# Source order for VectorE and ScalarE in the gated-input stage of a hybrid conformer layer, a softmax in two steps, and key and bias loads two heads ahead

## The chip, the cores and the metric

The kernel runs on one core of one Trainium2 chip. The time is device microseconds of one execution; the median of three runs of the kernel before is 1996.45 us (1996.19 to 1996.85). The engines are called as the profile calls them: PE (TensorE, matrix products), PEld (its weight loads), DVE (VectorE), ACT (ScalarE), POOL (GpSimd) and SP (SyncE, which here only issues DMAs).

## The reference

One layer of a streaming encoder, for a prompt of 256 frames and for 8 running streams of 16 new frames with 128 past frames each. Both share the weights.

```python
def hybrid_layer(x, conv_buf, ffn_buf, attn_fn, ...):
    h = rmsnorm(x, norm_mix_g)
    proj = h @ w_in            # [GLU in | q | k | v | forget logits | gate A | gate B]
    ...
    u = glu_in[..., :D_CONV] * jax.nn.sigmoid(glu_in[..., D_CONV:])
    ext = jnp.concatenate([conv_buf.astype(u.dtype), u], axis=1)
    z = layernorm(causal_dwconv(ext, conv_dw_w, conv_dw_b), conv_ln_g, conv_ln_b)   # 31 taps
    a_out = (z * jax.nn.sigmoid(z)) @ conv_pw_out
    q = rmsnorm(q, q_norm_g)
    k = rmsnorm(k, k_norm_g)
    logf = jax.nn.log_sigmoid(f_logit + b_forget)
    b_out = attn_fn(q, k, v, logf) @ w_att_out
    x = x + (gate_a * a_out + gate_b * b_out) @ w_out
    h2 = rmsnorm(x, norm_ffn_g)
    up = h2 @ w_up
    ...
    x = x + (jax.nn.silu(gc) * u_half) @ w_down
```

`attn_fn` is causal attention over 8 heads of 128 features. To each score a bias of summed log forget gates is added, and the softmax runs over the keys. The prompt is swept in two blocks of 128 queries; the 128 sample rows see their past keys (`cache_k`) and their own.

## The kernel before, in words

**Tokens and products.** The 256 + 128 = 384 tokens are three tiles of 128 rows. Every fp32 operand of a product is split into hi + lo, and each product is three matmuls (L245 to L247 with the weights stationary). Weights stream in as tiles `raw` of two 128-row blocks x 512 columns: SP issues the DMA (L139), ACT casts the high part `hi` (L148), and DVE forms the low part `lo` = raw - hi (L149). Of `raw`, `hi` and `lo` there are three buffers each.

**The gated-input stage.** `gemm` computes the GLU columns in four panels of 16 k-steps: 64 steps, 0 to 63. One weight tile serves two steps. At the first step of a tile, `ahead(3)` emits the fetch and split of the tile that is used two tiles later, so the split emitted at step 14 is used at steps 18 and 19. A panel ends at steps 15, 31, 47 and 63; its four PSUM results are evacuated by `glu_evac`: two by a DVE multiplication into `sgb` (L706) and a sigmoid on ACT (L707), which needs an ACT table load, two by a DVE multiplication into `ut` (L710), which POOL multiplies by `sgb` (L711).

**Beside it.** After each step, `tick` advances two generators.
- `attention()`: head h issues `head_operands` at step 6h + 6 (kTs, a DVE transposition of its past keys, L611, and qz, a DVE copy of its sample queries, L617), `head_scores` at 6h + 9, `head_probs` at 6h + 14, `head_out` at 6h + 17 and `head_last` at 6h + 19. `head_scores` fills three PSUM buffers s0 (L622), s1 (L624) and s2 (L626, and L630 against the past keys), adds the bias on DVE with the row's maximum (L636), negates (L638), and exponentiates on ACT (L639); before the change it also takes the reciprocal of the sum (L640, DVE) and scales (L641, ACT). `head_probs` transposes the probabilities on PE and copies them out of PSUM: pT on ACT (L650), pz on DVE (L653). `head_out` makes the outputs `on` (L665) and `attT` (L670), `head_last` the second `attT` (L676).
- `conv()`: the depthwise convolution, a chunk of 128 channels at a time, one DVE instruction for each of the 31 taps (L752, L754). Chunks overlap, so that in some steps two taps fall; `fill` (L731 to L737) builds a chunk's input, `load_state` fetches it.

**PSUM.** Products accumulate in five `acc` buffers; everything else rotates through three `misc` buffers. The scores of head h + 1 come one step behind `head_probs` of head h (steps 14 and 15, 20 and 21, 26 and 27, and so on to 50 and 51), and they take the buffers that `head_probs` leaves: s1 (L624) needs the one that pT (L650) reads, s2 (L626) the one that pz (L653) reads.

**What sets the order.** PE's order is written by hand: the order of the source. On the other engines a scheduler places instructions by priority, which is the source position less an offset: 150 for fetches and splits (SPLIT_AHEAD), 250 for the attention's steps (ATT_AHEAD), 400 for evacuations (EVAC_AHEAD). `queued(d)` ties an instruction behind the last queued one of its engine, without a wait. Key loads (`load_k`, four DMAs of a quarter each, two buffers) run one head ahead, bias loads (`load_b`, four DMAs) two. All loads, fetches among them, share SP's one queue, and each DMA waits there until its buffer is free.

Of the kernel before, what the change touches and what calls it, by code (L numbers as in the profile page):

```python
# [33 lines left out]
SPLIT_AHEAD, ATT_AHEAD, EVAC_AHEAD = 150, 250, 400  # L34
# [6 lines left out]
def hybrid_step(  # L41
# [70 lines left out]
    def newton_rsqrt(r, s, m):  # L112
        queued(nc.scalar.activation(s, m, AF.Sqrt), in_first())
        nc.vector.reciprocal(r, s)
# [31 lines left out]
    def split_rows(hi, lo, raw, o, k):  # L146
        first = in_first()
        queued(nc.scalar.copy(hi[:, k, :o], raw[:, k, :o]), first)  # L148
        queued(tt(lo[:, k, :o], raw[:, k, :o], f(hi[:, k, :o]), op=ALU.subtract), first)  # L149
# [77 lines left out]
    def gemm(jobs, sides=(), wide=False):  # L227
        for js in jobs:
# [4 lines left out]
            for j, k in [(j, k + i) for k in range(0, js[0]["nk"], 2) for j in js for i in range(2)]:  # L233
# [29 lines left out]
    def blocks(rows, put):  # L263
        src = rows.rearrange("p t (m b j) -> p b m t j", m=4, b=4)
        for b in range(4):
            for a in range(4):
                nc.vector.transpose(put(a, slice(32 * b, 32 * b + 32)), src[32 * a:32 * a + 32, b])  # L267
# [22 lines left out]
    def x_chunk(c):  # L290
# [5 lines left out]
        with tc.high_priority(offset=EVAC_AHEAD):  # L296
            queued(nc.scalar.activation(hi, ps[:, :NT], AF.Identity, scale=g))  # L297
# [4 lines left out]
    with tc.manual_schedule(engines={ENG.SP, ENG.Activation, ENG.DVE}):  # L302
        nc.vector.memset(junk[:, 0:1], 0.0)
        nc.scalar.dma_start(gm_row[:], norm_mix_g[0].rearrange("(c p) -> c p", p=P))
        nc.scalar.activation(junk[:, 1:2], junk[:, 0:1], AF.Identity)
# [16 lines left out]
        nc.vector.tensor_copy(gm[:], pv[:, :16])  # L322
# [17 lines left out]
    def over_partitions(dg, dst):  # L340
# [3 lines left out]
        nc.scalar.copy(dst, ps[:, :NT])  # L344
# [46 lines left out]
    def small_columns():  # L391
        ps = misc_tile()
        tr(ps[:, :R_N], vrow[:R_N, :], ident[:R_N, :R_N])
        nc.vector.tensor_copy(col[:], ps[:, :R_N])
        ts(qgs[:], col[:, R_QG:R_QG + 1], float(P) ** -0.5, None, op0=ALU.mult)

    def first_norm():
        for c in range(2, 16, 2):
# [6 lines left out]
            if c % 4 == 2:  # L405
                for t in range(NTT):
                    n = c // 4
                    sq = nc.scalar.activation(junk[:], xs[n][:, t, :], AF.Square, accum_out=ssx[:, t, n:n + 1])
# [9 lines left out]
        with tc.high_priority(offset=EVAC_AHEAD):  # L418
            nc.vector.tensor_reduce(mt[:], ssx[:], axis=mybir.AxisListType.X, op=ALU.add)
            ts(mt[:], mt[:], 1.0 / DM, EPS, op0=ALU.mult, op1=ALU.add)  # L420
            r = rsqrt(mt[:], [P, NTT], p_x0, "r1")
            nc.vector.tensor_copy(rs1[:], r[:])
# [14 lines left out]
    def tok_job(dst, c0, n, sq):  # L437
        d = job("B", 16, ha, tok_evac(dst, c0, n))

        def post():  # L440
            for t in range(NTT):
                for h in range(c0 // P, (c0 + n) // P):
                    jk = p_qkv.tile([P, P], F32, tag="jk", bufs=2, name="jk")
                    nc.scalar.activation(jk[:], dst[:, t, h * P:(h + 1) * P], AF.Square,
# [4 lines left out]
    def tok_evac(dst, c0, n, shared=True):  # L449
        def ev(t, ps):  # L450
            if shared and t % 2:
                ts(dst[:, t, c0:c0 + n], ps[:, :n], rs1[:, t:t + 1], None, op0=ALU.mult)
            else:
                queued(nc.scalar.activation(dst[:, t, c0:c0 + n], ps[:, :n], AF.Identity, scale=rs1[:, t:t + 1]),
# [16 lines left out]
    nc.scalar.activation(e[:], e[:], AF.Exp, scale=-1.0)  # L471
    ts(r[:], e[:], 2.0, None, op0=ALU.add)
    nc.vector.reciprocal(r[:], r[:])
# [27 lines left out]
    def bias_rows():  # L501
        for _ in range(6):
            yield
        for i in range(2):
# [3 lines left out]
            nc.vector.tensor_copy(cw[:, i * 124:(i + 1) * 124], ps[:, :124])  # L508
            nc.vector.tensor_copy(fw[:, i * 66:(i + 1) * 66], ps[:, 128:128 + 66])
# [5 lines left out]
        nc.scalar.activation(crow[:, :2 * P], ps[:H, :2 * P], AF.Copy, scale=-1.0)  # L515
        ps = misc_tile()
        mm(ps[:H, :P], lg[:, 2, :], bm[:], start=True, stop=True)
        nc.scalar.activation(crow[:, 2 * P:], ps[:H, :P], AF.Copy, scale=-1.0)
# [3 lines left out]
        nc.scalar.copy(drow[:], ps[:64, :P])  # L522
# [18 lines left out]
    def q_panel(n):  # L541
        blocks(qt[:, :, 512 * n:512 * (n + 1)], by_feature(attT[:, 4 * n:4 * n + 4]))
        for h in range(4 * n, 4 * n + 4):
            nc.scalar.activation(attT[:, h], attT[:, h], AF.Identity, scale=qgs[:])
# [64 lines left out]
    def head_past_keys(d):  # L609
        kTs = p_att.tile([P, 8, P], F32, tag="kTs", bufs=1, name="kTs")  # L610
        nc.vector.transpose(kTs[:].rearrange("p b k -> p (b k)"), kcs[d["h"]][:])  # L611
        d["kTs"] = kTs

    def head_operands(d):
        head_past_keys(d)
        d["bs"] = bss[d["h"]]
        nc.vector.tensor_copy(qz[d["h"] % 2][:, :, :, 0:16], by_stream(attT[:, d["h"], 2 * P:]))  # L617

    def head_scores(d):
# [14 lines left out]
        for i, (sp_, o, n) in enumerate(segs):  # L634
            v = pr[:, o * P:(o + n) * P]
            nc.vector.tensor_tensor_reduce(out=v, in0=sp_[:, :n * P], in1=bs[:, o * P:(o + n) * P], scale=1.0,  # L636
                                           scalar=-3.0e38, op0=ALU.add, op1=ALU.max, accum_out=mx[:, i:i + 1])
            ts(mx[:, 3 + i:4 + i], mx[:, i:i + 1], -1.0, None, op0=ALU.mult)  # L638
            nc.scalar.activation(v, v, AF.Exp, bias=mx[:, 3 + i:4 + i], accum_out=mx[:, 6 + i:7 + i])  # L639
            nc.vector.reciprocal(mx[:, i:i + 1], mx[:, 6 + i:7 + i])  # L640
# [466 lines left out]
```

## Time and profile before

| | us |
|---|---|
| median of 3 runs | 1996.45 |
| the profiled execution | 1998.56 |
| its span | 1996.7 |
| mean granted clock of PE | 0.999 |
| DVE, all additions of the split, L149 (x481) | 580.5 |
| ACT, all casts of the split, L148 (x481) | 496.3 |
| DVE, taps, L754 (x240) | 151.9 |

The profile is of one execution, so its times are set against 1998.56 and not against the median. A row of the timeline gives the start in us from the span's start, the length, the engine, the line, the operation, the output and inputs, and in brackets how long the engine had been idle and what released it. A window's row gives the busy time and instruction count of PE, PEld, DVE, ACT and POOL, then PE's granted clock (1.00 is full speed), the busy share of the 16 DMA engines (which can pass 1 where packets are counted together at an edge) and GB/s.

### The profile page before, as it was taken

To read this page: it belongs to the slowest core of one execution; us is meant where nothing else is said; L and a number is where in the kernel's file an instruction comes from. 1 tells how busy PE (TensorE), PEld (TensorE's weight loads), DVE (VectorE), ACT (ScalarE), POOL (GpSimd) and SP (SyncE) were. 2 spreads that over 40 slices of the span, in tenths; PEclk is the share of its full clock that TensorE was granted. 3 is DMA by queue.
4 is the path that set the end of the run, shared out by engine and by line. 5 is a ranking of instruction groups with operands and counts; after the bars stand their busy time and mean duration, and the time that the engine had idled before them with its cause. 6 is when DMAs were issued, how large, how long until landed. Compare 5 with 4: busy or idle time off the path is not lost.

```text
span 1996.7 us, 24449 instructions
## 1 busy us (share of the span) xinstructions
PE 1986.5 (99%) x9383; PEld 1676.0 (84%) x9383; DVE 1305.3 (65%) x1908; ACT 743.2 (37%) x1077; POOL 89.5 (4%) x216
## 2 busy tenths in 40 slices
PE   9999999999999999999999999999999999999999
PEld 9888999888888888888888888888888888888887
DVE  4455889788755487676867683377673376638663
ACT  5535354433334433344333432233332233323321
POOL 1000011100000000000000000010000000000000
PEclk9999999999999999999999999999999999999999
DMA  6564767444443334534344443444433444343443
GB/s 184 149 188 117 216 154 161 141 140 131 130 129 124 128 125 163 165 122 137 119 137 126 129 134 129 129 126 127 136 129 132 132 118 137 128 133 120 138 158 106
DMA packets 209254, 275.98 MB, mean 138 GB/s; under 512 B 55878, under 2 KB 96729, under 8 KB 209129
## 3 DMA queue, kind: packets, MB, share of 16 engines
q1 hardware_dynamic: 208817, 273.85, 46.0%
q8 instruction: 73, 1.20, 0.3%
q0 software_dynamic: 288, 0.57, 0.1%
q14 instruction: 44, 0.36, 0.1%
q10 hardware_dynamic: 32, 0.01, 0.0%
HBM read 266.98 MB, written 7.86 MB: 138 GB/s over the span
## 4 chain that ended last, share of the span: by engine, by line
PE 96%; DVE 2%; DMA 1%; issue 0%; SPq 0%; ACT 0%; DVEq 0%; ACTq 0%
PE acc L252 20%; PE acc L250 20%; PE acc L251 20%; PE misc L252 10%; PE misc L251 10%; PE misc L250 10%; PE acc L245 2%; PE acc L247 2%; PE acc L246 2%; DVE lo L149 1%; DMA raw<-in_w_in_dram 0%; DVE mixT L267 0%; DVE ut L754 0%; DMA vc<-in_cache_v_dram 0%; DMA bs<-c_dr 0%
## 5 line engine op out<-in xcount | busy, mean ns | idle before, releaser
L149 DVE TENSOR_TENSOR lo<-raw,hi 128x1024 fp32r<-128x1024 f32 (+2 forms) x481 | 580.5, 1207 | 530.7 <-ACT hi L148 526.8
L148 ACT CAST hi<-raw 128x1024 fp32r<-128x1024 f32 (+2 forms) x481 | 496.3, 1032 | 970.1 <-PE misc L252 841.1
L250 PE MATMUL acc<-hi,xg 128*128 128x512 f32 x704 | 274.9, 390 | 0.0
L252 PE MATMUL acc<-hi,xg 128*128 128x512 f32 x704 | 273.9, 389 | 0.0
L251 PE MATMUL acc<-lo,xg 128*128 128x512 f32 x704 | 273.9, 389 | 0.0
L250 PE MATMUL acc<-hi,hT 128*128 128x512 f32 (+1 forms) x512 | 193.0, 377 | 0.5 <-ACT hT L297 0.5
L252 PE MATMUL acc<-hi,hT 128*128 128x512 f32 (+1 forms) x512 | 190.4, 372 | 0.2
L251 PE MATMUL acc<-lo,hT 128*128 128x512 f32 (+1 forms) x512 | 190.3, 372 | 0.0
L250 PEld LDWEIGHTS acc<-hi,xg 128*128 128x128 f32 x704 | 132.1, 188 | 28.4
L754 DVE SCALAR_TENSOR_TENSOR ut<-ext,cw,ut 128x384 f32<-128x384 f32 x240 | 151.9, 633 | 6.0
L252 PEld LDWEIGHTS acc<-hi,xg 128*128 128x128 f32 x704 | 132.1, 188 | 27.5
L251 PEld LDWEIGHTS acc<-lo,xg 128*128 128x128 f32 x704 | 132.2, 188 | 27.1
L252 PE MATMUL misc<-hi,xg 128*128 128x512 f32 x352 | 137.0, 389 | 0.0
L250 PE MATMUL misc<-hi,xg 128*128 128x512 f32 x352 | 137.0, 389 | 0.0
L251 PE MATMUL misc<-lo,xg 128*128 128x512 f32 x352 | 136.9, 389 | 0.0
L250 PE MATMUL acc<-hi,act 128*128 128x512 f32 x352 | 136.9, 389 | 0.0
L251 PE MATMUL acc<-lo,act 128*128 128x512 f32 x352 | 136.9, 389 | 0.0
L252 PE MATMUL acc<-hi,act 128*128 128x512 f32 x352 | 136.9, 389 | 0.0
L267 DVE STREAM_TRANSPOSE extf<-tok 32x384 f32<-32x384 f32 x176 | 100.3, 570 | 30.9 <-ACT tok L988 28.2
L267 DVE STREAM_TRANSPOSE uT<-tok 32x384 f32<-32x384 f32 x176 | 100.3, 570 | 29.7 <-ACT tok L988 26.9
L250 PEld LDWEIGHTS acc<-hi,hT 128*128 128x128 f32 x512 | 96.2, 188 | 16.1 <-ACT hT L297 1.0
L252 PEld LDWEIGHTS acc<-hi,hT 128*128 128x128 f32 x512 | 96.1, 188 | 15.7 <-DVE hT L298 0.7
(325 smaller groups left out, 3133.8 us busy)
## 6 DMA issues: line engine op xcount, KB each, us to landing
raw<-in_w_up_dram SPq DMA_DIRECT2D x176, 512.0 KB
raw<-in_w_in_dram SPq DMA_DIRECT2D x96, 512.0 KB
raw<-in_w_down_dram SPq DMA_DIRECT2D x88, 512.0 KB
raw<-in_w_in_dram SPq DMA_DIRECT2D x64, 256.0 KB
raw<-in_w_out_dram SPq DMA_DIRECT2D x32, 512.0 KB
raw<-in_w_att_out_dram SPq DMA_DIRECT2D x16, 512.0 KB
raw<-in_conv_pw_out_dram SPq DMA_DIRECT2D x16, 512.0 KB
raw<-in_w_in_dram SPq DMA_DIRECT2D x23, 344.0 KB
```

What stands on the lines that cost most here:

```text
L148: queued(nc.scalar.copy(hi[:, k, :o], raw[:, k, :o]), first)
L149: queued(tt(lo[:, k, :o], raw[:, k, :o], f(hi[:, k, :o]), op=ALU.subtract), first)
L245: mm(o, hi[:, kk, s], ah, start=st, stop=False)
L246: mm(o, hi[:, kk, s], al, start=False, stop=False)
L247: mm(o, lo[:, kk, s], ah, start=False, stop=sp)
L250: mm(o, ah[:, s], hi[:, kk, :n], start=st, stop=False)
L251: mm(o, ah[:, s], lo[:, kk, :n], start=False, stop=False)
L252: mm(o, al[:, s], hi[:, kk, :n], start=False, stop=sp)
L267: nc.vector.transpose(put(a, slice(32 * b, 32 * b + 32)), src[32 * a:32 * a + 32, b])
L754: stt(o, v, wc, o, op0=ALU.mult, op1=ALU.add)
```

## The change

Four things change, and PE's order not at all.
- `dve` and `act` wrap VectorE and ScalarE. While the list `chained` isn't empty, each of their instructions is `queued`, that is, keeps its place in the source. The list is filled before the gated-input stage and emptied behind `drain(att_steps)`; evacuations in `gemm` are exempt. In the profile of the changed kernel all these instructions bear the line of the wrapper, L89.
- The softmax goes in two steps: `head_scores` ends with the exponentials, and a new `head_scale` at step 6h + 10 takes one reciprocal of three columns in place of three of one, and scales three times.
- The attention's steps lose their priority offset (ATT_AHEAD).
- Keys are loaded two heads ahead instead of one, bias loads move from `head_probs` to `head_scale`; these, the value loads and the convolution's state get the offset of the splits.

```diff
-SPLIT_AHEAD, ATT_AHEAD, EVAC_AHEAD = 150, 250, 400
+SPLIT_AHEAD, EVAC_AHEAD = 150, 400
...
+    chained = []
+
+    class InOrder:
+        def __init__(self, eng):
+            self.eng = eng
+
+        def __getattr__(self, name):
+            op = getattr(self.eng, name)
+
+            def call(*a, **kw):
+                d = op(*a, **kw)
+                if chained:
+                    queued(d)
+                return d
+            return call
+
+    dve, act = InOrder(nc.vector), InOrder(nc.scalar)
...
-    tt = nc.vector.tensor_tensor
-    stt = nc.vector.scalar_tensor_tensor
-    ts = nc.vector.tensor_scalar
+    tt = dve.tensor_tensor
+    stt = dve.scalar_tensor_tensor
+    ts = dve.tensor_scalar
...
                 if sp:
+                    held, chained[:] = chained[:], []
                     with tc.high_priority(offset=EVAC_AHEAD):
-                        for m in range(nb):
+                        for m in range(len(ps)):
                             j["evac"](m, ps[m])
+                    chained[:] = held
...
-            nc.scalar.activation(v, v, AF.Exp, bias=mx[:, 3 + i:4 + i], accum_out=mx[:, 6 + i:7 + i])
-            nc.vector.reciprocal(mx[:, i:i + 1], mx[:, 6 + i:7 + i])
-            nc.scalar.activation(v, v, AF.Identity, scale=mx[:, i:i + 1])
-        d["pr"] = pr
+            act.activation(v, v, AF.Exp, bias=mx[:, 3 + i:4 + i], accum_out=mx[:, 6 + i:7 + i])
+        d["pr"], d["mx"], d["segs"] = pr, mx, segs
+
+    def head_scale(d):
+        pr, mx = d["pr"], d["mx"]
+        dve.reciprocal(mx[:, 0:3], mx[:, 6:9])
+        for i, (_, o, n) in enumerate(d["segs"]):
+            v = pr[:, o * P:(o + n) * P]
+            act.activation(v, v, AF.Identity, scale=mx[:, i:i + 1])
...
-            for off, step in ((1, head_operands), (4, head_scores), (9, head_probs),
+            for off, step in ((1, head_operands), (4, head_scores), (5, head_scale), (9, head_probs),
                               (12, head_out), (14, head_last)):
...
-                with tc.high_priority(offset=ATT_AHEAD):
-                    step(d)
-                if step is head_operands and d["h"] + 1 < H:
-                    load_k(d["h"] + 1)
-                if step is head_probs and d["h"] + 2 < H:
-                    load_b(d["h"] + 2)
-                if step is head_probs and 0 < d["h"] < H - 1:
-                    load_v(d["h"] + 1)
+                step(d)
+                with tc.high_priority(offset=SPLIT_AHEAD):
+                    if step is head_operands and d["h"] + 2 < H:
+                        load_k(d["h"] + 2)
+                    if step is head_scale and d["h"] + 2 < H:
+                        load_b(d["h"] + 2)
+                    if step is head_probs and 0 < d["h"] < H - 1:
+                        load_v(d["h"] + 1)
...
                 if w == -16:
-                    load_state(c)
+                    with tc.high_priority(offset=SPLIT_AHEAD):
+                        load_state(c)
...
     load_k(0)
     load_b(0)
+    load_k(1)
     load_v(0)
     load_b(1)
     load_v(1)
     att_steps = attention()
+    chained.append(True)
     gemm([job("A", 16, ha, glu_evac(g)) for g in range(4)], [att_steps, conv_steps])
     drain(att_steps)
+    chained.clear()
```

The rest of the diff writes `dve.` and `act.` for `nc.vector.` and `nc.scalar.`.

How the instructions stand, at three places (`x2` is two in a row). **DVE around step 15**, the end of the first panel; first the kernel before, from the splits of steps 12 and 14 on (ISA is the bias addition with its maximum for head 1):

```order
L149 TENSOR_TENSOR lo<-raw,hi 128x1024 x2
L653 COPY pz_1992<-misc 128x8x16
L706 TENSOR_TENSOR sgb<-acc,rs1b 128x384 x2
L710 TENSOR_TENSOR ut<-acc,rs1b 128x384 x2
L636 ISA pr,mx<-misc,bs 128x128
```

The same place in the changed kernel:

```order
L89 TENSOR_TENSOR lo<-raw,hi 128x1024
L89 STREAM_TRANSPOSE kTs<-kc 128x1024
L89 COPY qz_1991<-attT 128x8x16
L89 TENSOR_TENSOR sgb<-acc,rs1b 128x384 x2
L89 TENSOR_TENSOR ut<-acc,rs1b 128x384 x2
L89 TENSOR_TENSOR lo<-raw,hi 128x1024
L89 COPY pz_1992<-misc 128x8x16
L89 ISA pr,mx<-misc,bs 128x128
```

The split of step 14 and the copy pz of head 0, which stood ahead of the four evacuations, now stand behind them. On ACT the cast of step 14 and the copy pT likewise stand behind the panel's two sigmoids now.

**SP around step 12**, the changed kernel (`kc` are quarters of a key load, `bs` the parts of a bias load, `raw` halves of weight tiles; the first four `kc` belong to head 2, the others to head 3):

```order
L156 DMA raw<-in_w_in_dram 128x2x256 x4
L606 DMA kc<-in_cache_k_dram 32x32x32 x4
L616 DMA bs<-c_dr 128x128
L617 DMA bs<-c_dr 128x256
L618 DMA bs<-c_dr 128x128
L619 DMA bs<-d_dr 128x1x128
L606 DMA kc<-in_cache_k_dram 32x32x32 x4
L156 DMA raw<-in_w_in_dram 128x2x256 x8
```

And the kernel before, where the bias load of head 2 and the first quarter of a key load come:

```order
L139 DMA raw<-in_w_in_dram 128x2x256 x2
L597 DMA bs<-c_dr 128x128
L598 DMA bs<-c_dr 128x256
L599 DMA bs<-c_dr 128x128
L600 DMA bs<-d_dr 128x1x128
L587 DMA kc<-in_cache_k_dram 32x32x32
```

Before, key quarters stand singly among the weight tiles; now eight of them and a bias load stand in one piece between two weight tiles. The second of these tiles is the one that the split of step 14 reads.

**DVE around step 51**, where the scores of head 7 come; before, from the split of step 50 on:

```order
L149 TENSOR_TENSOR lo<-raw,hi 128x1024
L754 SCALAR_TENSOR_TENSOR ut<-ext,cw,ut 128x384
L653 COPY pz_1992<-misc 128x8x16
L754 SCALAR_TENSOR_TENSOR ut<-ext,cw,ut 128x384
L149 TENSOR_TENSOR lo<-raw,hi 128x1024
L611 STREAM_TRANSPOSE kTs<-kc 128x1024
```

In the changed kernel, from the split of step 48 on:

```order
L89 TENSOR_TENSOR lo<-raw,hi 128x1024
L89 STREAM_TRANSPOSE kTs<-kc 128x1024
L89 COPY qz_1991<-attT 128x8x16
L89 SCALAR_TENSOR_TENSOR ut<-ext,cw,ut 128x384 x2
L89 COPY attT<-misc 128x128
L89 SCALAR_TENSOR_TENSOR ut<-ext,cw,ut 128x384 x2
L89 TENSOR_TENSOR lo<-raw,hi 128x1024
L89 COPY pz_1992<-misc 128x8x16
```

kTs of head 7 moves from behind the split of step 52 to behind that of step 48, and four taps stand between it and pz now. In the whole stage 61 taps stand on DVE instead of 85; the others come in the next stages.

More of the change, by code (lines that the diff above doesn't have):

```diff
@@ L147, in split_rows @@
         first = in_first()
-        queued(nc.scalar.copy(hi[:, k, :o], raw[:, k, :o]), first)
+        queued(act.copy(hi[:, k, :o], raw[:, k, :o]), first)
         queued(tt(lo[:, k, :o], raw[:, k, :o], f(hi[:, k, :o]), op=ALU.subtract), first)
@@ L793, in hybrid_step @@
         hi, lo = aHL[h // 4][:, 0, h % 4, :], aHL[h // 4][:, 1, h % 4, :]
-        nc.scalar.copy(hi, attT[:, h, :])
+        act.copy(hi, attT[:, h, :])
         tt(lo, attT[:, h, :], f(hi), op=ALU.subtract)
@@ L813, in layer_norm @@
         mm(ps[:, :NT], avg[:], sm[:], start=True, stop=True)
[L814 removed]
+        act.copy(mu, ps[:, :NT])
         yield
```

107 lines of the change are left out of this document (53 added, 54 removed).

## The prediction

> **What bounds the kernel now.** I read the page first, then the waits of PE, then the gated-input stage by windows, then the timeline around its one large wait. The page gives PE's share of the span and the chain that ended last; the waits answer gives, for each line that PE waited at, the sum, the number and the longest wait in us.
>
> ```profile
> PE 1986.5 (99%) x9383; PEld 1676.0 (84%) x9383; DVE 1305.3 (65%) x1908; ACT 743.2 (37%) x1077; POOL 89.5 (4%) x216
> PE 96%; DVE 2%; DMA 1%; issue 0%; SPq 0%; ACT 0%; DVEq 0%; ACTq 0%
> PE misc L630 <- DVE kTs L611: 2.5, 1, 2.5
> PE misc L317 <- POOL ident L109: 1.5, 1, 1.5
> 218.00:405.00 187.00, 184.50 (x1262) 174.79 (x1261) 155.87 (x322) 87.76 (x163) 21.64 (x29) 0.99 0.62 162
> ```
>
> PE is busy for 99% of the span and carries 96% of the chain. The whole program therefore holds only about 10 us in which PE does nothing. Only one wait of size lies where the change works: 2.5 us at L630, the scores against past keys, which waited for the transposed keys kTs. The last row is the window of the whole gated-input stage, 218 to 405 us (busy times of PE, PEld, DVE, ACT, POOL, then clock, DMA share, GB/s). PE is idle for 2.50 us of the 187.00: the wait at L630 is all there is to win. DVE is busy for 155.87 of them, 83%, so what stands behind what on DVE matters here.
>
> The timeline shows that wait (start, length, engine, line, operation; in brackets the idle time before and its releaser), in step 51, head 7:
>
> ```profile
> 349.72 1.04 ACT L148 CAST hi<-raw 128x1024 fp32r<-128x1024 f32 x1 [1.47 <-PE acc L246]
> 350.80 1.22 DVE L149 TENSOR_TENSOR lo<-raw,hi 128x1024 fp32r<-128x1024 f32 x1 [1.26 <-ACT hi L148]
> 351.94 1.24 DVE L611 STREAM_TRANSPOSE kTs<-kc 128x1024 f32<-128x1024 f32 x1
> 353.23 0.64 PE L630 MATMUL misc<-kTs,qz 128*32 128x128 f32 x16 [2.50 <-DVE kTs L611]
> 354.00:355.00 1.00, 1.00 (x5) 1.00 (x5) 0.71 (x7) 0.98 (x2) 0.00 (x0) 0.70 1.09 374
> 355.00:356.00 1.00, 1.00 (x4) 1.00 (x4) 0.11 (x1) 0.99 (x4) 0.00 (x0) 0.50 0.91 295
> 356.00:357.00 1.00, 1.00 (x4) 1.00 (x4) 0.05 (x1) 0.64 (x3) 0.00 (x0) 0.50 1.13 332
> 357.00:358.00 1.00, 1.00 (x5) 1.00 (x5) 0.00 (x0) 0.00 (x0) 0.00 (x0) 0.60 0.65 148
> ```
>
> The transposition of kTs stood on DVE behind a split (hi on ACT, then lo on DVE) that itself waited for PE. The four windows behind it show a second price: the granted clock was 0.70, 0.50, 0.50 and 0.60, so 0.3 + 0.5 + 0.5 + 0.4 = 1.7 us more were lost. The wait costs 2.5 + 1.7 = **4.2 us** in all. The Trainium skill ("TensorE: Matmul & The Clock Gate", section "What's actually happening") says that the clock falls to half after at least one idle window of about 3.4 us. Here 2.50 us of idleness was enough, so the trace decides; by the page's rule no stall below 3.4 us would touch the clock, every clock term below would go, and the sum would come to about +4.1 instead of +5.55.
>
> **The change, part by part.** PE's own order is the same before and after, so PE can gain or lose only by waits.
>
> *Removed: the wait at L630.* kTs of head 7 moves from behind the split of step 52 to behind that of step 48, three steps early: **-4.2 us**.
>
> *Step 9, head 0.* Now kTs and the copy qz stand behind the last transposes of the key panel (L267).
>
> ```profile
> 234.75 0.57 DVE L267 STREAM_TRANSPOSE qt<-kt 32x384 f32<-32x384 f32 x1
> 236.40 0.65 PE L630 MATMUL misc<-kTs,qz 128*32 128x128 f32 x16
> 240.42 0.21 DVE L617 COPY qz<-attT 128x128 f32<-128x128 f32 x1
> ```
>
> The last transpose ends at 235.32, then kTs (1.24) and qz (0.21): 236.77, where PE wants them at 236.40. **+0.35 us.**
>
> *Step 15, the first panel's end.* This is the main new cost. The evacuations are exempt from the chain and keep their high priority, the attention has lost its own, and so the evacuations now stand on DVE and ACT ahead of the split of step 14 and of head 0's copies pT and pz.
>
> ```profile
> 243.02 1.03 ACT L148 CAST hi<-raw 128x1024 fp32r<-128x1024 f32 x1
> 248.23 0.29 DVE L653 COPY pz<-misc 128x128 f32<-128x128 f32 x1
> 248.77 1.10 DVE L706 TENSOR_TENSOR sgb<-acc,rs1b 128x384 f32<-128x384 f32 x2 [0.24 <-PE acc L247]
> 249.83 1.08 DVE L710 TENSOR_TENSOR ut<-acc,rs1b 128x384 f32<-128x384 f32 x2
> 250.02 0.94 ACT L707 ACTIVATE sgb<-sgb 128x384 f32<-128x384 f32 x2
> 250.81 0.38 PE L626 MATMUL misc<-qt,attT 128*128 128x128 f32 x2
> 251.12 0.65 PE L630 MATMUL misc<-kTs,qz 128*32 128x128 f32 x16
> ```
>
> pz frees the buffer that L626, head 1's scores, writes at 250.81. Before, pz was done at 248.52. Now the evacuations must end first (250.91); the two sigmoids can start once the first sgb is there, so they end at about 250.3, the cast hi (1.04) at 251.35, lo (1.22) at 252.6, and pz (0.29) at 252.9. That is 2.1 us late even if the data are there: the lower end.
>
> They may not be there. On SP the key loads of heads 2 and 3 and a bias load now stand ahead of the weight tile that this split reads, and the load for head 3 waits until kTs of head 1 has freed its buffer, in chain behind the split at 243.02. What a load takes, from SP's issues and the DMA share (last but one column) of windows:
>
> ```profile
> 299.96 0.91 SPq L139 DMA_DIRECT2D raw<-in_w_in_dram  x2
> 301.00:302.00 1.00, 1.00 (x19) 0.80 (x20) 1.00 (x5) 0.98 (x1) 0.00 (x0) 1.00 0.76 212
> 302.00:303.00 1.00, 1.00 (x8) 1.00 (x7) 1.00 (x8) 0.89 (x4) 0.00 (x0) 1.00 0.93 309
> 303.00:304.00 1.00, 1.00 (x7) 1.00 (x6) 1.00 (x3) 0.51 (x2) 0.00 (x0) 1.00 0.03 10
> 304.44 0.47 SPq L587 DMA_DIRECT2D kc<-in_cache_k_dram  x1
> 305.00:306.00 1.00, 1.00 (x8) 0.93 (x6) 1.00 (x3) 0.85 (x3) 0.00 (x0) 1.00 0.80 171
> 306.00:307.00 1.00, 1.00 (x21) 0.75 (x20) 0.33 (x2) 0.87 (x3) 0.16 (x2) 1.00 1.43 268
> 307.00:308.00 1.00, 1.00 (x10) 1.00 (x9) 0.50 (x2) 0.78 (x2) 0.00 (x0) 1.00 0.74 210
> ```
>
> A weight tile whose issue ended at 300.87 keeps the DMA busy until about 303.0: it lands 2.1 us after its issue, with a share of 1.72. With one quarter of a key load the same takes 2.97, so a quarter costs up to 1.25 us, or 0.5 by its bytes (118 KB more at some 250 GB/s, an estimate). Four quarters are 2.0 to 5.0 us of DMA, of which 1.9 pass while they are issued (4 x 0.47): they hold a tile behind them back by 0.1 to 3.1.
>
> So: split of 243.02 done at 245.3 (1.03 + 1.22), kTs at 246.5, four key issues to 248.4, tile issued 249.3, landed 251.4, hi 252.4, lo 253.7, pz 254.0: **3.2 us** late with a bare transfer, 6.3 with the full load in front. I take 3.2, for it goes by the rows and lies between the ends. The clock: 0 to 1.7; I take 1.7, since the stall is longer than the 2.50 that cost it.
>
> *Step 27.* The key load of head 5, which waits for kTs of head 3 in step 24, now stands between the two halves of a weight tile that the split of step 26 reads. Counted from the end of the previous head's attT copy: lo 1.22, kTs 2.46, four issues 4.34, half a tile 4.79, landed 6.9, hi 7.9, lo 9.2, pz 9.4. The need is read from the same steps of head 5, below: copy ended 341.26, L626 of step 51 due at 350.42, so 9.16. Stall 0.3 to 3.4; I take **1.5**, towards the bare transfer, and clock 0 to 1.7, taken 0.8.
>
> *Step 51 again.* Before, DVE served pz early and kTs late. In source order two convolution taps stand in each step ahead of the attention's copies.
>
> ```profile
> 340.00 0.15 DVE L640 RECIPROCAL mx<-mx 128x1 f32<-128x1 f32 x1
> 340.07 0.27 DVE L665 COPY on<-misc 128x128 f32<-128x128 f32 x1
> 340.25 0.61 DVE L754 SCALAR_TENSOR_TENSOR ut<-ext,cw,ut 128x384 f32<-128x384 f32 x1
> 340.51 2.52 POOL L711 TENSOR_TENSOR ut<-ut,sgb 128x384 f32<-128x384 f32 x2 [8.48 <-ACT sgb L707]
> 340.84 0.42 DVE L670 COPY attT<-misc 128x256 f32<-128x256 f32 x1
> 341.18 2.26 DVE L754 SCALAR_TENSOR_TENSOR ut<-ext,cw,ut 128x384 f32<-128x384 f32 x2
> ```
>
> From 340.07, when the evacuations are over, DVE does three lo (3.66), a reciprocal (0.15), eight taps (4.88), on, attT and the last attT copy (0.27 + 0.42 + 0.27), kTs 1.24, qz 0.21 and pz 0.28: 11.38, so 351.45. PE came to L630 at 353.23 - 2.50 = 350.73, and to L626 0.31 earlier (251.12 less 250.81 in step 15), 350.42. Stall 1.0. While POOL multiplied, two taps took 2.26 instead of 1.22: 1.04 more if they fall together, 2.1 in all. I take **1.3**, near the plain sum, and clock 0 to 1.7, taken 0.6. The Trainium skill ("SBUF — State Buffer", section "Who interferes with whom") says that a DVE instruction with two SBUF inputs fully blocks while GpSimd reads SBUF. The row shows 1.04 us lost beside 2.52 us of POOL; by the page's rule the term would be 1.0 + 2.5 and the forecast 2.2 us higher.
>
> *Steps 31, 33 and 39* show 0 to 0.8 by the same reckoning; I take **0.3**, clock included.
>
> *At nothing:* 24 taps leave the stage (85 to 61 stand in it now), 24 x 0.61 = 15 us of DVE, into the next stages:
>
> ```profile
> 405.00:550.00 145.00, 145.00 (x645) 119.72 (x644) 121.69 (x172) 50.57 (x67) 5.23 (x10) 1.00 0.47 133
> 550.00:690.00 140.00, 139.85 (x622) 115.65 (x621) 75.59 (x103) 59.22 (x75) 1.02 (x1) 1.00 0.42 128
> ```
>
> DVE has 23 us free in the first and 64 in the second, and PE does not wait there; without that cover the 15 us would be PE's. Sixteen reciprocals fewer and scales one step later lie on DVE and ACT, four steps ahead of the transposes that read them: nothing.
>
> **Sum**: -4.2 + 0.35 + (3.2 + 1.7) + (1.5 + 0.8) + (1.3 + 0.6) + 0.3 = **+5.55 us**. The profiled execution took 1998.56 (its span 1996.7), 2.11 above the median of the runs, 1996.45; it would come to 2004.1, and the median to **2002.0**.
>
> **Rivals.**
> 1. *One stall for another* (not slower). Step 15 at its lower end, 2.1 + 1.7, and the DMA in time elsewhere: -4.2 + 0.35 + 3.8 = -0.05, 1996.4. For it: the bounds of steps 27 and 51 reach 0.3 and 1.0, and a tap or a copy that is moved by a microsecond hides these; against it: DVE's 83%. It decides whether weight tiles land before the sigmoids end, about 250.3.
> 2. *As the words have it*: nothing new waits, -3.85, 1992.6. Against it: the evacuations stand ahead of pz in the order itself, and 2.1 us follow from it whatever the data do.
> 3. *Key loads hold the weights back in full*: step 15 at 5.2 + 1.7, step 27 at 3.0 + 1.7: -3.85 + 6.9 + 4.7 + 1.9 + 0.3 = +9.95, 2006.4. For it: DMA shares of 1.09 to 1.43 beside key loads; against it: many tiles are fetched two splits ahead.
>
> **How the numbers follow.** Forecast 0.45 (its own range 1998 to 2007), rival 1 0.30, rival 2 0.05, rival 3 0.20. All terms at their low ends give -0.45, at their high ends +13.85. The range 1995.5 to 2009.5 leaves out rival 2 and the far end of rival 3. A measurement of this kernel can tell some 0.2%, 4.0 us, from no change. Slower by more: rival 3 and 0.37 of the forecast, 0.57. Within: rival 1, 0.08 of the forecast and 0.02 of rival 2, 0.40. Faster: 0.03.
>
> **What would show it.** In PE's waits of the changed kernel, no wait for kTs, and new ones at the score matmuls of steps 15, 27 and 51 for ACT's pT or DVE's pz; granted clocks of 0.5 to 0.7 in the windows behind them; key loads ahead of weight tiles on SP; 61 taps in the stage. I am wrong if PE's idle time in the stage is at or below 2.5 us, if the new waits name a weight DMA directly, or if PE waits appear behind 405 us, where the taps went.

## The result, and the profile after

The changed kernel takes 2008.3 us (median of 6 runs, 2007.27 to 2008.9) against 1996.68 for the kernel before (6 runs, 1996.19 to 1998.59): 11.6 us more, a ratio of 1.0056 with the interval 1.0043 to 1.0069. The forecast of 2002.0 had the direction right and half the size; the time lies within the range, 1.9 us beyond rival 3. The profiled execution took 2007.94 us with a span of 2005.8, so the two profiles differ by 9.1 us of span.

First the page of the changed kernel (busy shares, chain), then PE's waits, then the windows of the gated-input stage and of the stage behind it:

```profile
PE 1990.3 (99%) x9383; PEld 1677.8 (84%) x9383; DVE 1302.9 (65%) x1892; ACT 742.0 (37%) x1077; POOL 88.6 (4%) x216
PE 94%; DVE 3%; DMA 1%; issue 1%; SPq 1%; ACT 0%; DVEq 0%; ACTq 0%
PE misc L643 <- ACT pT L89: 6.4, 2, 4.6
PE misc L336 <- POOL ident L126: 1.5, 1, 1.5
PE misc L645 <- DVE pz L89: 1.2, 3, 0.6
PE misc L649 <- DVE qz L89: 0.2, 1, 0.2
218.00:405.00 187.00, 179.12 (x1219) 168.22 (x1218) 134.14 (x273) 83.00 (x153) 17.43 (x25) 0.97 0.61 157
405.00:550.00 145.00, 145.00 (x644) 119.78 (x643) 134.06 (x196) 50.53 (x70) 8.86 (x16) 1.00 0.48 134
```

The wait for kTs at L630 (now L649) is gone. In its place stand two waits for pT at L643, 4.6 and 1.8 us, three for pz, 1.2 in all, and the foreseen 0.2 for qz. PE is idle for 7.88 us of the stage's window instead of 2.50: 5.4 us more. Most of the rest of the loss is clock, 0.97 on the mean instead of 0.99. In the window behind the stage DVE has 12.4 us more to do (134.06 for 121.69), and PE still has no idle time.

The first wait, step 15, in the timeline of the changed kernel:

```profile
245.31 1.24 DVE L89 STREAM_TRANSPOSE kTs<-kc 128x1024 f32<-128x1024 f32 x1
246.58 2.20 SPq L606 DMA_DIRECT2D kc<-in_cache_k_dram  x4
248.75 1.10 DVE L89 TENSOR_TENSOR sgb<-acc,rs1b 128x384 f32<-128x384 f32 x2 [2.10 <-PE acc L264]
248.88 7.36 SPq L156 DMA_DIRECT2D raw<-in_w_in_dram  x7
249.35 1.06 ACT L89 ACTIVATE sgb<-sgb 128x384 f32<-128x384 f32 x2 [3.91 <-DVE sgb L89]
253.55 1.04 ACT L89 CAST hi<-raw 128x1024 fp32r<-128x1024 f32 x1 [3.14 <-DMA raw<-in_w_in_dram]
254.50 0.58 ACT L89 COPY pT<-misc 128x512 f32<-128x512 f32 x1
255.13 1.22 PE L643 MATMUL misc<-qt,attT 128*128 128x256 f32 x2 [4.61 <-ACT pT L89]
```

Read it from the bottom. L643 waits for pT; pT stands behind the cast hi; the cast, with ACT idle for 3.14 us after the sigmoids, waits for its weight tile; SP issued the tile only at 248.88, behind the key load of head 3, which could start when kTs of head 1 had freed its buffer (246.55). Windows around it show the traffic (DMA share and GB/s at the end of the row) and the clock behind the wait (the number before them):

```profile
249.00:250.00 1.00, 1.00 (x8) 1.00 (x7) 1.00 (x3) 0.64 (x2) 0.00 (x0) 1.00 1.46 176
250.00:251.00 1.00, 0.53 (x4) 0.33 (x2) 0.90 (x2) 0.41 (x1) 0.48 (x1) 1.00 1.52 147
252.00:253.00 1.00, 0.00 (x0) 0.00 (x0) 0.00 (x0) 0.00 (x0) 0.46 (x1) 1.00 1.08 375
253.00:254.00 1.00, 0.00 (x0) 0.00 (x0) 0.00 (x0) 0.45 (x1) 0.00 (x0) 0.67 1.10 387
255.00:256.00 1.00, 0.87 (x2) 0.50 (x2) 1.00 (x3) 0.98 (x2) 0.00 (x0) 0.50 0.62 216
257.00:258.00 1.00, 1.00 (x17) 0.58 (x17) 0.01 (x1) 0.60 (x2) 0.00 (x0) 0.50 0.88 251
259.00:260.00 1.00, 1.00 (x5) 1.00 (x5) 0.00 (x0) 1.00 (x3) 0.00 (x0) 0.50 0.09 27
```

While key quarters move, the DMA is full at 147 to 176 GB/s; with weights alone it moves 375. The Trainium skill ("DMA: Bandwidth & Descriptors", section "Why small descriptors are slow (HBM only)") names a fixed cost of every small packet as a cause of low rates; the rows agree in that keys, which come in rows of 128 bytes, fill the engines at less than half the rate, but they don't show the cost of one packet. The clock falls at 253.3, while PE still waits, and stays at 0.50 until 260. What PE loses of work by it is 0.4 in the window from 255, 0.5 in each of the four from 256 to 260 (two are shown) and 0.1 behind them, together 2.5 us. Step 15 cost 4.6 + 2.5 = 7.1. The next head's scores bear it out: head 1's start at 250.16 before and 250.14 now, head 2's 7.2 us later, the first row from the kernel before, the second from the changed one:

```profile
266.68 0.38 PE L622 MATMUL misc<-qt,attT 128*128 128x128 f32 x2
```

```profile
273.92 0.38 PE L641 MATMUL misc<-qt,attT 128*128 128x128 f32 x2
```

The second wait, step 27, has the same form: key load of head 5, then the second half of a weight tile, then the cast that waits for it.

```profile
285.20 2.14 SPq L606 DMA_DIRECT2D kc<-in_cache_k_dram  x4
287.38 0.69 SPq L156 DMA_DIRECT2D raw<-in_w_in_dram  x1
291.19 1.04 ACT L89 CAST hi<-raw 128x1024 fp32r<-128x1024 f32 x1 [8.44 <-DMA raw<-in_w_in_dram]
292.78 0.70 PE L643 MATMUL misc<-qt,attT 128*128 128x256 f32 x2 [1.76 <-ACT pT L89]
294.00:295.00 1.00, 1.00 (x18) 0.61 (x17) 0.96 (x6) 0.34 (x2) 0.00 (x0) 0.65 0.91 310
295.00:296.00 1.00, 1.00 (x7) 0.88 (x4) 0.80 (x7) 0.76 (x5) 0.00 (x0) 0.50 0.15 51
296.00:297.00 1.00, 1.00 (x5) 1.00 (x4) 0.48 (x1) 1.00 (x3) 0.00 (x0) 0.50 0.04 10
297.00:298.00 1.00, 1.00 (x6) 1.00 (x5) 0.44 (x1) 0.52 (x1) 0.00 (x0) 0.65 0.21 46
```

1.8 us for pT, 0.3 for pz behind it, and 0.35 + 0.5 + 0.5 + 0.35 = 1.7 of clock: 3.8.

### The profile page after: what moved, and what is told of

It is laid out like the page before. It is cut to its first block, busy times and chain, and to the rows that moved or that the text cites. A ratio compares the mean times of both kernels' runs of the same rounds, so it can differ in the third digit from the quotient of the medians.

```text
span 2005.8 us, 24436 instructions
## 1 busy us (share of the span) xinstructions
PE 1990.3 (99%) x9383; PEld 1677.8 (84%) x9383; DVE 1302.9 (65%) x1892; ACT 742.0 (37%) x1077; POOL 88.6 (4%) x216
## 4 chain that ended last, share of the span: by engine, by line
PE 94%; DVE 3%; DMA 1%; issue 1%; SPq 1%; ACT 0%; DVEq 0%; ACTq 0%
PE acc L267 20%; PE acc L269 20%; PE acc L268 20%; PE misc L268 10%; PE misc L269 10%; PE misc L267 10%; PE acc L262 1%; PE acc L263 1%; PE acc L264 1%; DMA raw<-in_w_in_dram 1%; DVE lo L89 1%; DVE qt L89 0%; DVE ut L89 0%; DVE mixT L89 0%; SPq L606 0%
## 5 line engine op out<-in xcount | busy, mean ns | idle before, releaser
L89 DVE TENSOR_TENSOR lo<-raw,hi 128x1024 fp32r<-128x1024 f32 (+2 forms) x481 | 579.3, 1205 | 542.1 <-ACT hi L89 538.1
L89 ACT CAST hi<-raw 128x1024 fp32r<-128x1024 f32 (+2 forms) x481 | 496.0, 1031 | 955.9 <-PE misc L269 827.9
L89 DVE SCALAR_TENSOR_TENSOR ut<-ext,cw,ut 128x384 f32<-128x384 f32 x240 | 148.7, 638 | 3.7
L89 DVE STREAM_TRANSPOSE extf<-tok 32x384 f32<-32x384 f32 x176 | 100.3, 570 | 30.9 <-ACT tok L89 28.2
L89 DVE STREAM_TRANSPOSE uT<-tok 32x384 f32<-32x384 f32 x176 | 100.3, 570 | 29.7 <-ACT tok L89 26.9
```

The costliest lines, as they stand in the source:

```text
L89: d = op(*a, **kw)
```

## The experiments

Two theories stood at the start. **A:** weight tiles are held back on SP and in the DMA by key loads, and what stands in order behind their splits is late. **B:** the order on DVE and ACT, evacuations ahead of pT and pz, makes the wait of step 15, and the transfer only coincides. Each comparison is with the kernel before on the same chip, whose median was 1998.0 to 1998.1 there.

| kernel | median us | before | difference | ratio, interval | waits of PE in the stage, profiled |
|---|---|---|---|---|---|
| keys one head ahead | 2001.45 | 1998.0 | +3.5 | 1.0019, 1.0011 to 1.0028 | 1.4 pT, 0.8 pz, 2.0 sgb, 0.3 qz |
| evacuations in the chain | 2009.93 | 1998.0 | +11.9 | 1.0063, 1.0051 to 1.0076 | 7.6 pT (two), 0.8 pz, 0.2 qz |
| both | 2000.59 | 1998.0 | +2.6 | 1.0014, 1.0005 to 1.0023 | 4.0 sgb, 0.2 pz, 0.2 qz |
| no chain | 2012.38 | 1998.0 | +14.4 | 1.0075, 1.0061 to 1.0089 | 12.1 lo (four) |
| three key buffers | 2002.13 | 1998.08 | +4.1 | 1.0019, 1.001 to 1.0028 | 1.4 pT, 0.4 pz, 3.0 sgb, 0.3 qz, 0.2 lo |
| loads as before, all chained | 1994.83 | 1998.08 | -3.3 | 0.9985, 0.9976 to 0.9993 | 0.2 qz |
| before + softmax in two steps | 1998.02 | 1998.08 | -0.1 | 1.0002, 0.9993 to 1.0011 | 2.5 kTs |
| before + kTs of head 7 first | 1994.45 | 1998.08 | -3.6 | 0.9983, 0.9974 to 0.9991 | none |
| two heads ahead, no priority, all chained | 1995.07 | 1997.99 | -2.9 | 0.9987, 0.9978 to 0.9996 | 0.2 qz |
| loads as before, evacuations exempt | 1995.96 | 1997.99 | -2.0 | 0.9991, 0.9983 to 1.0 | 0.6 pz, 0.2 qz |
| the change without the loads' priority | 1996.34 | 1998.04 | -1.7 | 0.9991, 0.9982 to 1.0 | 0.6 pz, 0.3 lo, 0.3 qz |

**Keys one head ahead.**

```diff
-                    if step is head_operands and d["h"] + 2 < H:
-                        load_k(d["h"] + 2)
+                    if step is head_operands and d["h"] + 1 < H:
+                        load_k(d["h"] + 1)
...
-    load_k(1)
```

> The changed kernel, but keys are loaded one head ahead again (no load of head 1 before the stage), so that no key load waits for kTs in front of a weight tile. Theory A (weight tiles held behind waiting key loads on SP make the long waits): step 27's 4.1 us go, and of step 15's 7.2 us (4.6 waited, the rest clock) only what the evacuations ahead of pT and pz cost by themselves is left, 1.6 to 2.1 us and 0 to 1.7 of clock: about 2000 us (1998.5 to 2002). Theory B (the evacuations' place on DVE and ACT makes step 15, the transfer only coincides): step 15 keeps its 7.2 us, 2004 to 2008.

2001.45, as A had it. The profile is of an execution of 2000.42, one of the fastest of the eleven, and the only one of them with a granted clock of 1.000; the others have 0.999 or 0.998. PE's waits in it:

```profile
PE acc L262 <- DVE sgb L89: 2.0, 1, 2.0
PE misc L643 <- ACT pT L89: 1.4, 1, 1.4
PE misc L645 <- DVE pz L89: 0.8, 2, 0.4
```

Step 15 keeps 1.4 us for pT and 0.4 for pz, which is what evacuations ahead of them cost with the tile in time (1.8 us; the prediction's lower end of 2.1 was 0.3 too high). Step 27 has no wait. But a new wait came that neither theory had: 2.0 us at the first matmul of the third panel, for sgb. Its origin, in the timeline of this kernel (the last row is a window):

```profile
289.28 0.62 SPq L619 DMA_DIRECT2D bs<-d_dr  x1
290.00 0.92 SPq L156 DMA_DIRECT2D raw<-in_w_in_dram  x2
290.96 5.50 SPq L606 DMA_DIRECT2D kc<-in_cache_k_dram  x4
296.17 1.05 ACT L89 CAST hi<-raw 128x1024 fp32r<-128x1024 f32 x1 [3.85 <-DMA raw<-in_w_in_dram]
297.25 1.23 DVE L89 TENSOR_TENSOR lo<-raw,hi 128x1024 fp32r<-128x1024 f32 x1 [2.85 <-ACT hi L89]
298.39 1.24 DVE L89 STREAM_TRANSPOSE kTs<-kc 128x1024 f32<-128x1024 f32 x1
299.55 0.98 DVE L89 TENSOR_TENSOR sgb<-acc,rs1b 128x384 f32<-128x384 f32 x2
291.00:292.00 1.00, 1.00 (x14) 0.88 (x16) 0.53 (x2) 0.89 (x3) 0.00 (x0) 1.00 0.38 97
```

Here the tile was issued ahead of the four key quarters and still landed 5.2 us after its issue (290.92 to 296.17) instead of the 2.1 of a tile alone. The keys behind it can't be the whole cause. Right in front of it stood a bias load (its last part is the first row); between 291 and 292 the DMA was only 0.38 busy; and among the DMA packets of the trace the first of the keys starts at 293.49, 2.6 us after the tile's issue, while those of the bias load run until 292.9. lo, kTs and then the evacuations stood in one row behind the tile.

**Evacuations in the chain.**

```diff
-                    held, chained[:] = chained[:], []
                     with tc.high_priority(offset=EVAC_AHEAD):
...
-                    chained[:] = held
```

> The changed kernel, but the evacuations are in the chain too, so that the split of step 14, pT and pz stand ahead of them again; the loads as changed. Theory A: the weight tile still lands at about 253.5 us, so the wait for pT of 4.6 us and its clock stay: 2007 to 2009 us. Theory B: step 15's 7.2 us go, 2001 us.

2009.93: B falls. With pz and pT ahead of the evacuations the longest wait for pT is still 4.3 us:

```profile
PE misc L641 <- ACT pT L89: 7.6, 2, 4.3
PE misc L643 <- DVE pz L89: 0.8, 1, 0.8
```

So at step 15 two things were late at once, and the later one, the tile, set the wait.

**Both edits.**

> Both: keys one head ahead, evacuations in the chain. Both theories: the waits of steps 15 and 27 go, 2008.3 - 7.2 - 4.1 = 1997 us, or less by what the wait for kTs of head 7 cost the kernel before beyond the 1.2 us that steps 9, 45 and 51 cost now: 1994 to 1997.5 us. If chaining has another cost, above 1998.

2000.59, above what both theories said. The waits of steps 15 and 27 are gone, but the one for sgb that the first run showed is 4.0 us here:

```profile
PE acc L262 <- DVE sgb L89: 4.0, 1, 4.0
```

With keys one head ahead the loads thus still hurt; so A was right about the tiles but wrong that the wait for kTs is the only way. The chained evacuations alone don't explain it: a later run has them too, and not this wait.

**No chain.**

```diff
-    chained.append(True)
```

> The changed kernel without the chain (the list stays empty); loads two heads ahead and the softmax in two steps stay, the scheduler orders DVE and ACT. kTs of head 1 then stands ahead of the split of step 12, pz ahead of the evacuations, and the key loads between weight tiles. Theory A, with the chain as what makes the key load wait: no wait of more than 1 us in the stage but perhaps one for pz in step 51, 1994 to 1999 us. If loads two heads ahead cost by their traffic alone: 2003 to 2008 us.

2012.38, a miss for both numbers: without the chain it is slower still. PE waits four times for lo itself, 12.1 us; in the first of these places:

```profile
PE acc L264 <- DVE lo L89: 12.1, 4, 4.3
270.58 0.92 SPq L156 DMA_DIRECT2D raw<-in_w_in_dram  x2
271.59 6.48 SPq L606 DMA_DIRECT2D kc<-in_cache_k_dram  x4
278.31 1.05 ACT L89 CAST hi<-raw 128x1024 fp32r<-128x1024 f32 x1 [4.35 <-DMA raw<-in_w_in_dram]
```

A tile landed 6.8 us after its issue, with four key quarters right behind it (and again a bias load right in front, issued from 268.54 to 270.48), and the next tile was issued only at 278.18. The chain isn't what hurts; the loads are, and the scheduler's order hides them no better.

**Three key buffers.**

```diff
-        kc = kcs[h] = p_att.tile([P, 8 * P], F32, tag="kc", bufs=2, name="kc")
+        kc = kcs[h] = p_att.tile([P, 8 * P], F32, tag="kc", bufs=3, name="kc")
```

> The changed kernel with three key buffers instead of two, so that a key load two heads ahead doesn't wait for kTs. If that wait held the weight tile back, step 15 falls from 4.6 us to some 1.5 to 2 and step 27's wait goes: 2000 to 2003 us. If loading two heads ahead costs by its traffic, the time stays at 2006 to 2010.

2002.13, within the first range: with the third buffer six issues of tile halves in a row begin at 242.26, ahead of kTs of head 1 (245.50) instead of behind it, and the long waits of steps 15 and 27 are gone. What is left is the 1.4 us of the evacuations' place and 3.0 us at the third panel's start, as with keys one head ahead. It also changed where the loads stand on SP (key quarters on both sides of the bias load), so it doesn't part the buffer from the place.

**Loads as before, everything chained.** Keys one head ahead, evacuations in the chain, and no priority for any load (the bias loads stay in `head_scale`, where the change put them):

```diff
...
-                with tc.high_priority(offset=SPLIT_AHEAD):
-                    if step is head_operands and d["h"] + 2 < H:
-                        load_k(d["h"] + 2)
-                    if step is head_scale and d["h"] + 2 < H:
-                        load_b(d["h"] + 2)
-                    if step is head_probs and 0 < d["h"] < H - 1:
-                        load_v(d["h"] + 1)
+                if step is head_operands and d["h"] + 1 < H:
+                    load_k(d["h"] + 1)
+                if step is head_scale and d["h"] + 2 < H:
+                    load_b(d["h"] + 2)
+                if step is head_probs and 0 < d["h"] < H - 1:
+                    load_v(d["h"] + 1)
...
-                    with tc.high_priority(offset=SPLIT_AHEAD):
-                        load_state(c)
+                    load_state(c)
```

> Everything in the chain, evacuations too, the softmax in two steps, but key loads one head ahead and all loads without priority, as in the kernel before (key quarters stand singly between weight tiles at first). Theory A, now with the collision of four key quarters in a row with a weight tile as what makes the waits (also the one of 4.0 us for the evacuations that the run with both edits showed at the end of the second panel): that wait goes or falls below 1 us, 1 to 4 us faster than before. Theory C (the chain itself puts the evacuations behind whatever waits, whatever the loads do): the wait at the second panel's end stays, 2 to 4 us slower than before.

1994.83, 3.3 us faster than before; the wait for sgb is gone. Against the run with both edits, only the loads' priority differs: it cost 5.9 us there (+2.6 against -3.3, on two chips). Theory C falls. Four quarters in a row still occur here:

```profile
276.51 0.92 SPq L156 DMA_DIRECT2D raw<-in_w_in_dram  x2
277.47 7.46 SPq L604 DMA_DIRECT2D kc<-in_cache_k_dram  x4
```

They take 7.46 us to issue, and PE waits for nothing behind them. So it isn't a key load in one piece as such that costs; it costs where a tile beside it is due.

**The softmax alone.** The kernel before with `head_scale` as in the change.

> The kernel before with the softmax in two steps alone (one reciprocal of three columns, scales one step later). Priced at nothing: within 1.5 us of before on the same chip, with the wait for kTs of head 7 as before. If the later scales delay pT and pz, a wait at a score matmul appears and it is 2 us slower or more.

1998.02 against 1998.08: nothing, as priced, and the wait for kTs is unchanged.

**kTs of head 7 first.** The kernel before and one dependency more:

```diff
-    newest = {}
+    newest, keys_first = {}, []
...
-        nc.vector.transpose(kTs[:].rearrange("p b k -> p (b k)"), kcs[d["h"]][:])
+        t_ = nc.vector.transpose(kTs[:].rearrange("p b k -> p (b k)"), kcs[d["h"]][:])
+        if d["h"] == H - 1:
+            queued(t_, False)
+            keys_first.append(True)
...
-        queued(tt(lo[:, k, :o], raw[:, k, :o], f(hi[:, k, :o]), op=ALU.subtract), first)
+        queued(tt(lo[:, k, :o], raw[:, k, :o], f(hi[:, k, :o]), op=ALU.subtract), first or bool(keys_first))
+        keys_first.clear()
```

> The kernel before, with one order more: kTs of head 7 is queued ahead of the low part of step 50's split on DVE. If the wait for kTs was a cost of its own, PE no longer waits 2.5 us there, nor is the clock cut behind it: 2.5 to 4.2 us faster than before on the same chip. If another wait stands right behind it (pz, or the delayed split), within 1 us of before.

1994.45, the fastest of all: 3.6 us less than before. The two largest waits that are left in the whole program lie outside the stage:

```profile
PE misc L318 <- POOL ident L109: 1.5, 1, 1.5
PE misc L888 <- DVE sgA L882: 0.5, 2, 0.3
```

This prices the wait that the change set out from: 3.6 us in these medians, where the prediction took 4.2 from one execution.

**Two heads ahead without priority, everything chained.** The run with loads as before and everything chained, but `load_k(d["h"] + 2)` and `load_k(1)` as in the change.

> Everything in the chain, evacuations too, keys loaded two heads ahead as in the change, but all loads without priority. The key load of head 3, which waits for kTs of head 1, then stands one weight tile later on SP, behind the tile that step 14's split reads. If what costs is that a load waits in front of a tile that is due, the wait of step 15 goes and step 27 has 0 to 2 us left: 2 us faster to 2 us slower than before. If two heads ahead costs wherever it stands: 5 us slower than before or more.

1995.07, 2.9 us faster than before: loading two heads ahead costs next to nothing (0.4 us against the run with loads as before) where the loads stand behind the tile that is due.

**Loads as before, evacuations exempt.**

> Loads wholly as before, the chain as in the change with the evacuations exempt, the softmax in two steps. With the loads as before the scheduler puts pz ahead of the first panel's evacuations by itself, and the same for ACT. If exempting them costs something of its own, slower than the run with everything in the chain and the loads as before; if not, within 1 us of it, 2 to 4 us faster than before.

1995.96, 2.0 faster than before (the interval just reaches 1.0), 1.1 slower than with the evacuations in the chain (medians of two chips, so only roughly). What its profile shows more than that run's is one wait of 0.6 us for pz, in step 51. The bias loads stay in `head_scale` here too. In its order on DVE the split of step 14 and pz stand ahead of the evacuations:

```
L89 TENSOR_TENSOR lo<-raw,hi 128x1024
L89 COPY pz_1992<-misc 128x8x16
L89 TENSOR_TENSOR sgb<-acc,rs1b 128x384 x2
L89 TENSOR_TENSOR ut<-acc,rs1b 128x384 x2
```

**The change without the loads' priority.** Everything else of the change stays: keys two heads ahead, the chain, the exempt evacuations.

```diff
-                with tc.high_priority(offset=SPLIT_AHEAD):
-                    if step is head_operands and d["h"] + 2 < H:
-                        load_k(d["h"] + 2)
+                if step is head_operands and d["h"] + 2 < H:
+                    load_k(d["h"] + 2)
...
-                    with tc.high_priority(offset=SPLIT_AHEAD):
-                        load_state(c)
+                    load_state(c)
```

> The changed kernel less one thing: the loads of keys, biases, values and the convolution's state have no priority. Two heads ahead, the chain, the exempt evacuations and the softmax in two steps stay. Without the priority the scheduler puts the split of step 14, pT and pz ahead of the first panel's evacuations again. If the priority is the whole cost, 1 to 3.5 us faster than before, with at most waits below 1 us for pz at steps 45 and 51. If the exempt evacuations or two heads ahead cost of themselves, slower than before.

1996.34, 1.7 us faster than before (its interval just reaches 1.0), where the whole change is 11.6 slower. The waits that are left:

```profile
PE misc L645 <- DVE pz L89: 0.6, 1, 0.6
PE acc L268 <- DVE lo L89: 0.3, 1, 0.3
```

The order on DVE at step 15 is the one printed just above. So the priority of the loads is the one part whose removal alone turns the loss into a gain: it costs 1.7 + 11.6, some 13 us (the two differences are of two chips). It does so together with the loads two heads ahead, for with keys one head ahead it cost less, 5.9 us in the pair of runs above. Keys, biases, values and states lose the priority at once in these runs, so how much each of them costs is not shown.

## Why the prediction was right in direction and short by half

| step of the sum | forecast | profiled | |
|---|---|---|---|
| wait at L630 goes | -2.5 and -1.7 clock | gone | right; -3.6 in the medians of the run that removes it alone |
| step 9 | +0.35 | 0.2 | right |
| step 15 | +3.2 and +1.7 | 4.6 and 2.5 | too small by 2.2 |
| step 27 | +1.5 and +0.8 | 2.1 and 1.7 | too small by 1.5 |
| step 51 | +1.3 and +0.6 | 0.6 and 0 | too large by 1.3 |
| steps 31, 33, 39 | +0.3 | none; 0.3 in step 45 | right in size, by luck: in another step |
| taps, reciprocals | 0 | 0 | right: the softmax alone does nothing, the taps cost DVE 12.4 us and PE none |
| sum | +5.55 | +7.8 by these rows, +9.1 by the spans | medians +11.6; 1.3 of the spans' difference stays unassigned |

**The mis-sized term** is that of step 15, and in the same way step 27: I took a bare transfer, 2.1 us from issue to landing, although four key quarters stood right in front of the tile, and kept the full load only for rival 3. The split's cast began at 253.55, where the working had the tile landed at 251.4. The issue was forecast complete at 249.3; the trace has the two halves issued from 248.88 to 250.07, 0.8 later. The transfer then took 3.5 us instead of 2.1, 1.4 more. Rival 3, at 2006.4, had mechanism and size and got a chance of 0.20. Its 5.2 us for step 15 aren't the 6.3 that the working gives for the full load; with the upper ends of steps 15 and 27 it would have come to 2007.9. A row that spoke for it was already quoted: a DMA share of 1.43 beside a single quarter.

**The wait was named at the wrong instruction.** I let pz at L626 bind; pT at L643 did, since PE asks for it first and it comes behind the same cast.

**The clock term** was read from one wait of 2.50 us and put at 1.7 for any longer one. The wait of 4.61 lost 2.5. Waits of 1.4 and 2.0 us, in the profiled execution with keys one head ahead, lost nothing; its windows around the 2.0 us keep a clock of 1.00 (the number after POOL):

```profile
299.00:300.00 1.00, 0.00 (x0) 0.00 (x0) 1.00 (x3) 0.00 (x0) 0.00 (x0) 1.00 1.06 356
301.00:302.00 1.00, 1.00 (x8) 0.96 (x7) 1.00 (x2) 1.00 (x2) 0.85 (x1) 1.00 1.07 335
```

The other ten executions of that kernel, with clocks of 0.999 or 0.998, took 1.1 us more on the median (2001.5), so the same waits may well lose clock in them. The term is thus not a fixed price of a wait.

**A reason was wrong though its number held.** The prediction put the evacuations ahead of pz down to their exemption and to the attention's lost priority. The last two runs keep both and have pz first. What moved them was the loads' priority, which is all that differs between the last run and the change. The likely reason, which no run shows by itself, is that with key loads ahead of the tile on SP the scheduler expects the split of step 14 late and lets the evacuations pass. One edit thus made both the late tile and the order that looked like a second cause. The run with evacuations in the chain shows that this order added little beside the tile.

**Step 51** had 0.6 us instead of 1.3. From the end of the evacuations to pz DVE took 11.4 us (351.99 to 363.34), as reckoned, though two of the eight taps fell beside POOL and took 2.58 (the other pairs 1.13 or 1.14): they lost some 1.4 us beside 2.89 us of POOL, not all of it. But PE asked for the buffer 10.8 us after the evacuations (362.76) and not 10.35, as read from the kernel before, where the evacuations had started late behind a tap.

**What stays open.** The medians differ by 11.6, the two profiled executions by 9.4 (2007.94 and 1998.56). That of before lies 1.9 above its median. That the clock is cut behind the wait of 2.5 us in some executions only would explain it; its runs spread over 3.5 us (1995.71 to 1999.19) and those of the kernel without that wait over 1.3. The granted clocks of the single runs speak for it: of the 90 runs of the kernel before beside the experiments, 54 have a clock of 0.999 and a median of 1998.4, and 36 have 1.000 and 1997.1, while in the kernel without the wait the two groups have the same median. With the cut in 54 of 90 runs the wait would cost 2.5 + 0.6 x 1.7 = 3.5 us, an estimate near the 3.6 measured. No trace shows it: the clocks are rounded to a thousandth, which is 2 us here, and both profiles with that wait show the cut. The 1.3 us of the spans that the rows leave out stay unexplained.

## What to carry to other kernels

- A load that is given the priority of the work it competes with is not just earlier: it stands in front of the transfer that is due next. Give priority to what is due, and put early loads behind it.
- Where small-row and large-row transfers share a queue, price the large one by a row that shows both together, not by a row of it alone, and look at what stands in front of it as well as behind it.
- Before a late order on an engine is blamed, see whether the scheduler chose it because of a load: undo the load first, and read the order again.

## What the runs showed of the hardware that was not expected

A weight tile of 512 KB took 2.1 us from issue to landing alone, 3.5 behind a key load of 512 KB (step 15), and 5.2 and 6.8 us between a bias load of 320 KB in front and a key load behind it. In these last two cases no packet of the keys had started in the first 2.6 us after the tile's issue, a time in which a tile alone is through. So what stood in front of the tile had its part in the delay as well as what came behind; no run parts the two.

Issuing four quarters took SP 2.14 to 7.46 us, and everything behind them on SP waited that long. What sets this time is not shown: the 7.46 us came behind a bias load and a tile, with the DMA only 0.15 and 0.33 busy in the first two windows (277 to 279).

The clock cuts that the profiles show behind these waits come in two sizes. After the waits of 2.5 us (kernel before), 1.8 and 0.3 (step 27) and 3.0 us (three key buffers) the windows' shortfalls from 1.00 add up to 1.7 us, which at half clock is 3.4 us of cut; after the 4.6 us (step 15) and the 4.0 us for sgb they add up to 3.4, or 6.8 us of cut, of which 2.5 and 3.0 fell on work. In the kernel before the cut began 1.2 us after PE was at work again (354.4 and 353.23), at step 15 while it still waited. The 2.0 us for sgb had no cut in the one execution profiled. The Trainium skill ("TensorE: Matmul & The Clock Gate", section "What's actually happening") describes a free-running window of about 3.4 us behind the cut. The length of the cuts agrees with it; that waits of 2.5 us and of 1.8 with 0.3 behind it were enough for one doesn't fit a rule that a whole window must be idle.
